# Latent queries projected in six blocks of 128 rows, the turned rows once, multiplied by cosine and sine as they leave PSUM

## The chip, the cores and the metric

The kernel runs on one core of one Trainium2 chip, alone. The metric is the device time of one execution in microseconds (us), the median of several runs. Three runs of the kernel before took 1103.07, 1103.22 and 1104.04 us, so the median is 1103.22.

Five engines work side by side, each through its own list of instructions in a fixed order: PE multiplies matrices (its weight loads are listed as PEld), DVE and ACT do work on whole tiles, POOL issues DMAs and a few small operations, SP issues DMAs. An instruction that needs a result of another engine waits on a semaphore, and everything behind it on its own engine waits too.

## What is computed

A trunk of two layers over 512 tokens of width 1024, in float32; each layer is a mixer followed by a gated FFN with a short convolution. The change touches the first layer's latent attention (MLA), which has 8 heads. Of each head's 96 query columns 64 are used as they are ("nope") and 32 are turned by the rotary embedding:

```python
def rope(x, pos):
    half = x.shape[-1] // 2
    ...
    x1, x2 = xf[..., :half], xf[..., half:]
    return jnp.concatenate([x1 * cos - x2 * sin, x2 * cos + x1 * sin], axis=-1)
...
q = heads_first(rms_norm(c_q, cq_g) @ w_uq, MLA_HEADS)
q_nope, q_rope = q[..., :MLA_NOPE], rope(q[..., MLA_NOPE:], pos)
kv = heads_first(rms_norm(c_kv, ckv_g) @ w_ukv, MLA_HEADS)
k_nope, v_mla = kv[..., :MLA_NOPE], kv[..., MLA_NOPE:]
o_mla = mla_attention(q_nope, q_rope, k_nope, rope(k_rope, pos), v_mla)
```

Scores are q_nope·k_nope + q_rope·k_rope, scaled by 96^-0.5, masked to the past, turned into shares by a softmax, and multiplied with the values. All heads share one turned key k_rope.

## The kernel before

Tokens are tiled in four blocks of 128 (`NT`), contraction dimensions in pieces of 128 (`P`). A product in float32 is made of three passes over split operands, high·high, high·low and low·high (`mm3`, lines 321 to 325): hence three rows, L323 to L325, for every product. Weights come in by DMA (`wraw`) and are split by ACT (`wh`, a cast, L84) and DVE (`wl`, a subtraction, L85); a split reuses the buffer of the weights split some steps earlier.

The first layer runs in stages. First the input projection makes, for each token, 256 latent query numbers, 128 latent key/value numbers and 32 key numbers to be turned (tile `ac`). A token-major tile `ctok` takes the normalised latents in its first three blocks of 128 columns; in the fourth it takes the turned key, four times over. PE transposes the four blocks into `tc`, and ACT and DVE split the first three into `cth` and `ctl` and put the turned key rows into `mk` (L1106 to L1109). Then the latent stage, the loop over `p2` (L1121 to L1142): in each of its four passes two heads' queries (`auq`), their keys (`auk`, 128 rows for two heads) and one token block of values (`auv`) are projected, each into a bank of PSUM under tag "a". Three banks have that tag, so a projection waits until an earlier one has been read out.

A head's query block before has 128 rows: 64 nope rows, the 32 rows to be turned, and the same 32 again with halves exchanged. DVE multiplies the whole block by a table `qtab` (one, cosine, sine, and the scale) as it leaves PSUM: one instruction for a head, L1128, eight in all, into `mq`. Score products run over 128 rows, and the key tile `mk` holds the turned key twice, so that cosine part and sine part add up in the product. In even heads the nope rows lie at 0 to 63, in odd heads at 64 to 127. ACT copies `auk` to `mk` (L1136, L1137, 64 rows each) and `auv` to `mv` (L1142).

The attention loop follows (L1226 to L1243): 16 units n, pair of heads p2 = n // 4, token block i = n % 4. For unit n PE makes two score tiles `sps` (L1151, the two banks of tag "s"); DVE adds the mask and takes the extreme (L1155); ACT takes exponentials (L1158); DVE takes reciprocals and scales (L1164, L1166); PE transposes the shares of unit n - 1 (`tpp`, L1178), DVE and ACT copy them out (L1189, L1187); after the last token block of a pair PE multiplies with the values (L1196). Between these, `plan` puts pieces of another projection, `av` for the differential attention (L1206, again tag "a"), on PE as a filler. In this loop the order on PE, DVE and ACT is as the code writes it; in the latent stage and ahead of it a scheduler sets the order of each engine when the kernel is built, and gives each projection one of the free banks.

Of the kernel before, what the change touches and what calls it, by code (L numbers as in the profile page):

```python
# [9 lines left out]
F32 = mybir.dt.float32  # L10
F32R = mybir.dt.float32r
BF16 = mybir.dt.bfloat16
AF = mybir.ActivationFunctionType
ALU = mybir.AluOpType
# [3 lines left out]
P = 128  # L18
S = 512
# [79 lines left out]
def trunk(tc, A, out):  # L99
# [3 lines left out]
    with ExitStack() as top:  # L103
# [103 lines left out]
        units += [(A["ev_w_uq"][u], 1024) for u in range(2)] + [(A["ev_w_ukv"], 1024)]  # L207
# [654 lines left out]
        def even():  # L862
            with ExitStack() as es:
# [43 lines left out]
                with ExitStack() as e1:  # L907
# [3 lines left out]
                    mv = mp.tile([P, NT, 512], F32, tag="mv", name="mv")  # L911
                    e2 = ExitStack()
# [152 lines left out]
                    with e2:  # L1065
                        qtab = cp.tile([P, 2, S], F32, tag="qtab", name="qtab")
# [11 lines left out]
                        for i in ORDER:  # L1078
# [4 lines left out]
                            for k in range(KD) if i < 2 else ():  # L1083
# [13 lines left out]
                            DVE.tensor_tensor(ctok[:, 3].rearrange("p (a b) -> p a b", a=4),  # L1097
                                              ra[:, 0:1].to_broadcast([P, 4, 32]),
                                              ra[:, 1:2].to_broadcast([P, 4, 32]), ALU.add)
# [9 lines left out]
                            ACT.copy(mk[1][0:64, t], tp[0:64, 3])  # L1109
# [10 lines left out]
                        kvh, kvl = W.next()  # L1120
                        for p2 in range(4):  # L1121
                            for z in range(2):
                                h = 2 * p2 + z
                                acc = bank("a", "auq")
                                for k in range(2):
                                    mm3(acc[:], uq[k][0][:, h * P:(h + 1) * P], uq[k][1][:, h * P:(h + 1) * P],
                                        ch[:, k], cl[:, k], k == 0, k == 1)
                                DVE.tensor_tensor(mq[h][:], acc[:], qtab[:, z], ALU.mult)  # L1128
                            he, ho = mk[2 * p2], mk[2 * p2 + 1]
                            if p2:  # L1130
                                DVE.tensor_copy(he[64:128, :], mk[0][64:128, :])
                                DVE.tensor_copy(ho[0:64, :], mk[1][0:64, :])
                            acc = bank("a", "auk")
                            mm3(acc[:], kvh[:, p2 * P:(p2 + 1) * P], kvl[:, p2 * P:(p2 + 1) * P],
                                ch[:, 2], cl[:, 2], True, True)
                            ACT.copy(he[0:64, :], acc[0:64, :])  # L1136
                            ACT.copy(ho[64:128, :], acc[64:128, :])  # L1137
                            i = p2
                            t = slice(i * P, (i + 1) * P)
                            acc = bank("a", "auv")  # L1140
                            mm3(acc[:], ch[:, 2, t], cl[:, 2, t], kvh[:, 512:], kvl[:, 512:], True, True)
                            ACT.copy(mv[:, i], acc[:])  # L1142
# [77 lines left out]
                    scored, left = {}, []  # L1220

# [4 lines left out]
                    with tc.manual_schedule(engines={PE.engine, DVE.engine, ACT.engine}):  # L1226
                        for n, (before, behind) in enumerate(plan):
# [9 lines left out]
                            if n < len(units):  # L1237
                                shares(scored[n])
                            fill(behind)
# [694 lines left out]
def layout(inputs):  # L1934
# [23 lines left out]
    nope, x1, x2 = uq[:, :, :64], uq[:, :, 64:80], uq[:, :, 80:]  # L1958
    even = np.concatenate([nope, x1, x2, x2, x1], 2)
    odd = np.concatenate([x1, x2, x2, x1, nope], 2)  # L1960
    uq = np.where((np.arange(8) % 2 == 0)[None, :, None], even, odd)
    r["ev_w_uq"] = uq.reshape(2, P, 1024)
# [36 lines left out]
    te = np.concatenate([one, c2.T, s2.T], 0) * sc  # L1999
    to = np.concatenate([c2.T, s2.T, one], 0) * sc  # L2000
    r["rope_q"] = np.stack([te, to], 1).astype(f)
# [32 lines left out]
```

## Time and profile before

| what | value |
|---|---|
| runs | 1103.07, 1103.22, 1104.04 us |
| profiled execution, first to last instruction (span) | 1101.2 us |
| median of the runs less that span | 2.0 us |
| PE: first query block of the latent stage starts | 42.65 us |
| PE: first filler product `av` starts | 59.64 us |
| PE: first score product of the next attention starts | 113.45 us |

The profile gives the profiled execution by its span alone; times in it are us from the start of the span. A timeline row reads: start, duration, engine, line, operation, out<-in, shape, count; in brackets the idle time of the engine in front of it and what ended that. A row with x2 or more merges instructions that follow each other.

### The profile page before, as it was taken

The numbers are of one execution on the slowest core, as the hardware profiler recorded it, in microseconds if no ns is written. First come the engines' busy times: TensorE is split into PE (matmuls) and PEld (weight loads), VectorE is DVE, ScalarE is ACT, GpSimd is POOL, SyncE is SP. The second block draws the span as 40 slices with busy tenths as digits, with TensorE's granted clock in tenths as the row PEclk, the third lists the DMA queues.
The fourth block names the chain that finished last, engine by engine and source line by source line (L and its number), as shares of the span: only waits on it lengthen the run. The fifth ranks groups of instructions, "written<-read, shape, count | busy, mean of one in ns | idle before, by whom it ended". The sixth has DMA issues, their size and how long they took to land.

```text
span 1101.2 us, 18064 instructions
## 1 busy us (share of the span) xinstructions
PE 1092.6 (99%) x6736; PEld 957.5 (87%) x6736; DVE 902.1 (82%) x1519; ACT 647.2 (59%) x1104; POOL 127.9 (12%) x246
## 2 busy tenths in 40 slices
PE   9999999999999999999999999999999999999997
PEld 8876788898999999888888877789999999988886
DVE  6766786498999999998974765468899999999896
ACT  6555676346666665556644654555566666656562
POOL 3211134220000000000032111114100000000002
PEclk9999999999999999999999999999999999999999
DMA  7897898467555555345618999867655555535462
GB/s 275 257 246 217 217 307 230 115 185 203 171 184 192 178 180 178 125 162 172 233 56 286 271 298 301 242 181 237 199 165 192 174 182 183 188 119 180 142 203 77
DMA packets 72601, 217.51 MB, mean 198 GB/s; under 512 B 10049, under 2 KB 11201, under 8 KB 64321
## 3 DMA queue, kind: packets, MB, share of 16 engines
q1 hardware_dynamic: 61872, 147.99, 40.2%
q0 software_dynamic: 9920, 67.12, 24.0%
q10 hardware_dynamic: 720, 1.25, 0.4%
q8 instruction: 53, 0.87, 0.3%
q14 instruction: 36, 0.29, 0.1%
HBM read 208.95 MB, written 73.43 MB: 256 GB/s over the span
## 4 chain that ended last, share of the span: by engine, by line
PE 96%; DVE 2%; ACT 1%; issue 0%; POOL 0%; POOLq 0%; DVEq 0%; ACTq 0%
PE u L325 12%; PE u L324 12%; PE u L323 12%; PE acc L324 6%; PE acc L323 6%; PE acc L325 6%; PE apt L323 3%; PE apt L324 3%; PE apt L325 3%; PE ao L323 2%; PE ao L325 2%; PE ao L324 2%; PE aqk L323 1%; PE p L325 1%; PE p L324 1%; PE p L323 1%
## 5 line engine op out<-in xcount | busy, mean ns | idle before, releaser
L85 DVE TENSOR_TENSOR wl<-wraw,wh 128x1024 fp32r<-128x1024 f32 x246 | 298.2, 1219 | 36.9 <-ACT wh L84 36.6
L84 ACT CAST wh<-wraw 128x1024 fp32r<-128x1024 f32 x246 | 254.3, 1046 | 100.1 <-PE u L324 22.1
L325 PE MATMUL u<-xh,wl 128*128 128x256 f32 (+1 forms) x640 | 194.9, 305 | 0.0
L324 PE MATMUL u<-xl,wh 128*128 128x256 f32 (+1 forms) x640 | 194.7, 304 | 0.0
L323 PE MATMUL u<-xh,wh 128*128 128x256 f32 (+1 forms) x640 | 194.5, 305 | 0.0
L325 PEld LDWEIGHTS u<-xh,wl 128*128 128x128 f32 x640 | 122.3, 191 | 5.5 <-DVE wl L85 0.7
L324 PEld LDWEIGHTS u<-xl,wh 128*128 128x128 f32 x640 | 122.3, 191 | 4.9
L323 PEld LDWEIGHTS u<-xh,wh 128*128 128x128 f32 x640 | 122.2, 191 | 5.0
L323 PE MATMUL u<-gh,wh 128*128 128x256 f32 x384 | 108.7, 283 | 0.0
L325 PE MATMUL u<-gh,wl 128*128 128x256 f32 x384 | 108.6, 283 | 0.0
L324 PE MATMUL u<-gl,wh 128*128 128x256 f32 x384 | 108.6, 283 | 0.0
L324 PE MATMUL acc<-wl,gh 128*128 128x512 f32 (+1 forms) x234 | 90.8, 388 | 0.0
L325 PE MATMUL acc<-wh,gl 128*128 128x512 f32 (+1 forms) x234 | 90.7, 387 | 0.0
L323 PE MATMUL acc<-wh,gh 128*128 128x512 f32 (+1 forms) x234 | 90.2, 388 | 0.0
L236 POOL TENSOR_TENSOR rv<-ms,epst 128x1 f32<-128x1 f32 x31 | 12.4, 399 | 615.6 <-ACT junk L290 285.0
L487 ACT ACTIVATE y<-u,cw 128x512 f32<-128x512 f32 x88 | 67.5, 776 | 27.2 <-PE u L325 27.2
L324 PEld LDWEIGHTS u<-gl,wh 128*128 128x128 f32 x384 | 73.7, 192 | 0.1
L323 PEld LDWEIGHTS u<-gh,wh 128*128 128x128 f32 x384 | 73.6, 192 | 0.1
L325 PEld LDWEIGHTS u<-gh,wl 128*128 128x128 f32 x384 | 73.7, 192 | 0.0
L164 POOL DMA_DIRECT2D ws<-in_ffn_up_q x72 | 51.5, 720 | 154.9 <-DMA ws<-ws 77.5
L493 DVE SCALAR_TENSOR_TENSOR y<-u,cw,y 128x510 f32<-128x510 f32 x88 | 65.6, 747 | 2.2
L491 DVE SCALAR_TENSOR_TENSOR y<-u,cw,y 128x511 f32<-128x511 f32 x88 | 65.1, 743 | 0.0
(391 smaller groups left out, 2475.6 us busy)
## 6 DMA issues: line engine op xcount, KB each, us to landing
ws<-in_ffn_up_q POOLq DMA_DIRECT2D x48, 768.0 KB, 12.9
wraw<-ws SPq DMA_DIRECT2D x128, 256.0 KB, 2.9
wraw<-in_ffn_up_q SPq DMA_DIRECT2D x96, 256.0 KB, 2.9
wraw<-in_ffn_w_down SPq DMA_DIRECT2D x44, 512.0 KB, 3.5
ws<-ws POOLq DMA_DIRECT2D x16, 768.0 KB, 13.3
ws<-in_ffn_up_q POOLq DMA_DIRECT2D x24, 512.0 KB, 6.3
wraw<-in_ffn_w_up SPq DMA_DIRECT2D x24, 512.0 KB, 4.4
wraw<-in_od_w_dqk SPq DMA_DIRECT2D x12, 512.0 KB, 9.6
```

The source lines that it names most:

```text
L84: self.nc.scalar.copy(h[:, :w], raw[:, :w])
L85: self.nc.vector.tensor_tensor(l[:, :w], raw[:, :w], h[:, :w].bitcast(F32), ALU.subtract)
L164: nc.gpsimd.dma_start(tiles[j][c][:].rearrange(wide, q=4), src.rearrange(wide, q=4), accum_op=op, max_dma_last_dim=8192)
L236: POOL.tensor_tensor(v[:, :n], ms, eps[:, :n], ALU.add)
L323: PE.matmul(o, lh, rh, start=first, stop=False, skip_group_check=more)
L324: PE.matmul(o, lh, rl, start=False, stop=False, skip_group_check=more)
L325: PE.matmul(o, ll, rh, start=False, stop=last, skip_group_check=more)
L487: ACT.activation(y[:, z], u[z], AF.Identity, bias=c[:, 3:4], scale=c[:, 2:3])
L491: DVE.scalar_tensor_tensor(y[:, z, 1:], u[z][:, :S - 1], c[:, 1:2], y[:, z, 1:], ALU.mult, ALU.add)
L493: DVE.scalar_tensor_tensor(y[:, z, 2:], u[z][:, :S - 2], c[:, 0:1], y[:, z, 2:], ALU.mult, ALU.add)
```

## The change

Query rows are laid out in six blocks of 128 in place of eight: for four heads together, two blocks that hold 64 nope rows, the 32 rows to be turned of that head and the 32 of a head two further on, and one block with the nope rows of two heads. The rows to be turned are projected once. DVE multiplies them twice, by the cosine into rows 64 to 95 of `mq` and by the sine into rows 96 to 127; the key tile has the turned key and, below it, the turned key with halves exchanged (one more small copy by ACT into `ctok` for each token block). All heads now have nope rows at 0 to 63. The nope block is taken out by ACT with the scale. For the second four heads ACT copies the two blocks to `q_late` in SBUF, and the eight DVE multiplications of these run inside the attention loop, one in each of units 0, 1, 2, 4, 5, 6, 8 and 9. `qtab` and `q_late` lie in buffers that the first layer's later attention uses afterwards.

```diff
@@ -204,7 +204,7 @@
         units = []
         units += [(A["ev_w_c"][u], 832) for u in range(4)]
         units += [(A["ev_w_dqk"][0, 0], 1024), (A["ev_w_dqk"][0, 1], 1024)]
-        units += [(A["ev_w_uq"][u], 1024) for u in range(2)] + [(A["ev_w_ukv"], 1024)]
+        units += [(A["ev_w_uq"][u], 768) for u in range(2)] + [(A["ev_w_ukv"], 1024)]
         units += [(A["ev_w_dv"][u], 1024) for u in range(4)]
         for h in range(1, 4):
             units += [(A["ev_w_dqk"][h, z], 1024) for z in range(2)]
@@ -909,6 +909,8 @@
                     mq = [mp.tile([P, S], F32, tag=f"mq{h}", name=f"mq{h}") for h in range(8)]
                     mk = [mp.tile([P, S], F32, tag=f"mk{h}", name=f"mk{h}") for h in range(8)]
                     mv = mp.tile([P, NT, 512], F32, tag="mv", name="mv")
+                    qtab, q_late = [ap.tile([P, 2, S], F32, tag=f"dqk{n}", name=name)
+                                    for n, name in ((2, "qtab"), (3, "q_late"))]
                     e2 = ExitStack()
                     cp = e2.enter_context(tc.tile_pool(name="ec", bufs=1, reuse_waits="tile"))
                     cgain = cp.tile([P, 384], F32, tag="cgain", name="cgain")
@@ -1063,7 +1065,6 @@
                         split_qk()
 
                     with e2:
-                        qtab = cp.tile([P, 2, S], F32, tag="qtab", name="qtab")
                         cT = (cp.tile([P, 3, S], F32R, tag="cth", name="cth"),
                               cp.tile([P, 3, S], F32R, tag="ctl", name="ctl"))
                         wc = [W.next() for _ in range(4)]
@@ -1094,9 +1095,10 @@
                                                      ALU.mult, ALU.mult)
                             DVE.scalar_tensor_tensor(ra[:, 1, 16:32], a[:, 384:400], ri, rtab[:, i, 1, 16:32],
                                                      ALU.mult, ALU.mult)
-                            DVE.tensor_tensor(ctok[:, 3].rearrange("p (a b) -> p a b", a=4),
-                                              ra[:, 0:1].to_broadcast([P, 4, 32]),
-                                              ra[:, 1:2].to_broadcast([P, 4, 32]), ALU.add)
+                            DVE.tensor_tensor(ctok[:, 3, 0:96].rearrange("p (a b) -> p a b", a=3),
+                                              ra[:, 0:1].to_broadcast([P, 3, 32]),
+                                              ra[:, 1:2].to_broadcast([P, 3, 32]), ALU.add)
+                            ACT.copy(ctok[:, 3, 96:128], ctok[:, 3, 16:48])
                             DVE.scalar_tensor_tensor(cf[:, 0:256], a[:, 0:256], rq[:, 0:1], cgain[:, 0:256],
                                                      ALU.mult, ALU.mult)
                             DVE.scalar_tensor_tensor(cf[:, 256:384], a[:, 256:384], rk[:, 0:1], cgain[:, 256:],
@@ -1106,7 +1108,6 @@
                                 PE.transpose(tp[:, k], ctok[:, k], ident[:])
                             split(cT[0][:, :, t], cT[1][:, :, t], tp[:, 0:3])
                             ACT.copy(mk[0][64:128, t], tp[64:128, 3])
-                            ACT.copy(mk[1][0:64, t], tp[0:64, 3])
                         row = bank("o", "row")
                         for i in range(NT):
                             PE.transpose(row[:, i * P:(i + 1) * P], r_tok[:, i:i + 1].to_broadcast([P, P]), ident[:])
@@ -1118,23 +1119,46 @@
                         ch, cl = cT
                         uq = [W.next() for _ in range(2)]
                         kvh, kvl = W.next()
+                        turned_q = []
+
+                        def q_block(g, b):
+
+                            acc = bank("a", "auq")
+                            c = slice((3 * g + b) * P, (3 * g + b + 1) * P)
+                            for k in range(2):
+                                mm3(acc[:], uq[k][0][:, c], uq[k][1][:, c], ch[:, k], cl[:, k], k == 0, k == 1)
+                            h = 4 * g + b
+                            if b == 2:
+                                for z in range(2):
+                                    ACT.activation(mq[h + z][0:64, :], acc[z * 64:(z + 1) * 64, :], AF.Copy,
+                                                   scale=-(96 ** -0.5))
+                                return
+                            src = acc
+                            if g:
+                                src = q_late[:, b]
+                                ACT.copy(src, acc)
+                            lo, hi = slice(64, 96), slice(96, 128)
+                            steps = [lambda o=o, r=r, n=n: DVE.tensor_tensor(o, src[r], qtab[r, n], ALU.mult)
+                                     for o, r, n in ((mq[h][0:96, :], slice(0, 96), 0), (mq[h][hi, :], lo, 1),
+                                                     (mq[h + 2][lo, :], hi, 0), (mq[h + 2][hi, :], hi, 1))]
+                            if g:
+                                turned_q.append(steps)
+                            else:
+                                for step in steps:
+                                    step()
+
                         for p2 in range(4):
-                            for z in range(2):
-                                h = 2 * p2 + z
-                                acc = bank("a", "auq")
-                                for k in range(2):
-                                    mm3(acc[:], uq[k][0][:, h * P:(h + 1) * P], uq[k][1][:, h * P:(h + 1) * P],
-                                        ch[:, k], cl[:, k], k == 0, k == 1)
-                                DVE.tensor_tensor(mq[h][:], acc[:], qtab[:, z], ALU.mult)
+                            for b in ((0, 1), (2, ))[p2 % 2]:
+                                q_block(p2 // 2, b)
                             he, ho = mk[2 * p2], mk[2 * p2 + 1]
-                            if p2:
-                                DVE.tensor_copy(he[64:128, :], mk[0][64:128, :])
-                                DVE.tensor_copy(ho[0:64, :], mk[1][0:64, :])
+                            for x in (he, ho):
+                                if x is not mk[0]:
+                                    DVE.tensor_copy(x[64:128, :], mk[0][64:128, :])
                             acc = bank("a", "auk")
                             mm3(acc[:], kvh[:, p2 * P:(p2 + 1) * P], kvl[:, p2 * P:(p2 + 1) * P],
                                 ch[:, 2], cl[:, 2], True, True)
                             ACT.copy(he[0:64, :], acc[0:64, :])
-                            ACT.copy(ho[64:128, :], acc[64:128, :])
+                            ACT.copy(ho[0:64, :], acc[64:128, :])
                             i = p2
                             t = slice(i * P, (i + 1) * P)
                             acc = bank("a", "auv")
@@ -1218,6 +1242,7 @@
                     units = [(p2, i) for p2 in range(4) for i in range(NT)]
                     plan = [(3, 0), (1, 0), (1, 0), (2, 0)] + [(3, 0), (0, 1), (1, 0), (2, 0)] * 3 + [(2, 2), (0, 0)]
                     scored, left = {}, []
+                    late_q = [turned_q[b][n] for n in range(4) for b in range(2)]
 
                     def fill(n):
                         for _ in range(n):
@@ -1236,6 +1261,8 @@
                                 turn(*units[n - 1], scored.pop(n - 1)[0])
                             if n < len(units):
                                 shares(scored[n])
+                            if n in (0, 1, 2, 4, 5, 6, 8, 9):
+                                late_q.pop(0)()
                             fill(behind)
                             if n == 8:
                                 W.ahead(W.pos + 1)
@@ -1955,11 +1982,10 @@
     r["ev_w_dqk"] = np.stack([cols(w[:, 416:928], P), cols(w[:, 928:1440], P)], 1)
     r["ev_w_dv"] = rows(w[:, 1440:], 2)
     uq = a["ev_w_uq"][0].reshape(256, 8, 96)
-    nope, x1, x2 = uq[:, :, :64], uq[:, :, 64:80], uq[:, :, 80:]
-    even = np.concatenate([nope, x1, x2, x2, x1], 2)
-    odd = np.concatenate([x1, x2, x2, x1, nope], 2)
-    uq = np.where((np.arange(8) % 2 == 0)[None, :, None], even, odd)
-    r["ev_w_uq"] = uq.reshape(2, P, 1024)
+    nope, turn = uq[:, :, :64], uq[:, :, 64:]
+    r["ev_w_uq"] = np.concatenate([part for h in (0, 4) for part in (
+        nope[:, h], turn[:, h], turn[:, h + 2], nope[:, h + 1], turn[:, h + 1], turn[:, h + 3],
+        nope[:, h + 2], nope[:, h + 3])], 1).reshape(2, P, 768)
     ukv = a["ev_w_ukv"][0].reshape(P, 8, 2, 64)
     r["ev_w_ukv"] = ukv.transpose(0, 2, 1, 3).reshape(P, 1024)
     r["ev_w_out"] = rows(a["ev_w_out"][0], 1)
@@ -1996,9 +2022,9 @@
     r["rope_tok"] = np.stack([c2, s2], 1).reshape(NT, P, 2, 32).transpose(1, 0, 2, 3).astype(f)
     sc = -(96 ** -0.5)
     one = np.ones((64, S))
-    te = np.concatenate([one, c2.T, s2.T], 0) * sc
-    to = np.concatenate([c2.T, s2.T, one], 0) * sc
-    r["rope_q"] = np.stack([te, to], 1).astype(f)
+    tc = np.concatenate([one, c2.T, c2.T], 0) * sc
+    ts = np.concatenate([one, -s2.T, -s2.T], 0) * sc
+    r["rope_q"] = np.stack([tc, ts], 1).astype(f)
     p = np.arange(P)[:, None]
     dist = p - (np.arange(S)[None, :] - 384)
     r["mla_mask"] = np.where(dist >= 0, 0.0, BIG).astype(f)
```

The order of instructions, at three places. A number behind a name tells buffers of one name apart; `mq0` to `mq7` are the heads' query tiles, `mk0` to `mk7` their key tiles.

PE, first pass of the latent stage, before: keys, values, then the next head's queries (`sps`, the score product, comes only after the whole stage).

```order
L323 MATMUL auk_696<-cth_353,wh_595 128x512
L324 MATMUL auk_696<-ctl_354,wh_595 128x512
L325 MATMUL auk_696<-cth_353,wl_596 128x512
L323 MATMUL auv_702<-wh_595,cth_353 128x512
L324 MATMUL auv_702<-wl_596,cth_353 128x512
L325 MATMUL auv_702<-wh_595,ctl_354 128x512
L323 MATMUL auq_707<-cth_353,wh_369 128x512
```

The same place in the change:

```order
L323 MATMUL auk_704<-cth_354,wh_596 128x512
L324 MATMUL auk_704<-ctl_355,wh_596 128x512
L325 MATMUL auk_704<-cth_354,wl_597 128x512
L1175 MATMUL sps_794<-mk0_125,mq0_117 128x128
L323 MATMUL auv_710<-wh_596,cth_354 128x512
L324 MATMUL auv_710<-wl_597,cth_354 128x512
L325 MATMUL auv_710<-wh_596,ctl_355 128x512
L323 MATMUL auq_715<-cth_354,wh_370 128x512
```

The first score product of head 0 has moved into the stage, between keys and values; that of head 1 stands at the same place of the second pass.

ACT, end of the latent stage and first exponential of the attention loop, before (`wh` are the last weights that `av` needs):

```order
L1142 COPY mv_133<-auv_760 128x512
L84 CAST wh_670<-wraw_668 128x1024
L84 CAST wh_676<-wraw_674 128x1024
L1136 COPY mk6_131<-auk_783 64x512
L1137 COPY mk7_132<-auk_783 64x512
L1142 COPY mv_133<-auv_789 128x512
L1158 ACTIVATE s_805,st_804<-s_805,st_804 128x128
```

The same place in the change:

```order
L1139 COPY q_late_135<-auq_737 128x512
L1139 COPY q_late_135<-auq_745 128x512
L1160 COPY mk4_129<-auk_755 64x512
L1161 COPY mk5_130<-auk_755 64x512
L1166 COPY mv_133<-auv_761 128x512
L84 CAST wh_671<-wraw_669 128x1024
L84 CAST wh_677<-wraw_675 128x1024
L1133 ACTIVATE mq6_123<-auq_766 64x512
L1133 ACTIVATE mq7_124<-auq_766 64x512
L1160 COPY mk6_131<-auk_777 64x512
L1161 COPY mk7_132<-auk_777 64x512
L1166 COPY mv_133<-auv_783 128x512
```

Two copies are new in front of the casts, and behind them two instructions that read the last query block, `auq_766`.

DVE, units 0 and 1 of the attention loop, in the change (before, the rows with `q_late` are not there, and the others stand in the same order; ISA rows are the masking step and its result):

```order
L1190 TENSOR_SCALAR s_799<-s_799,st_798 128x128
L1190 TENSOR_SCALAR s_800<-s_800,st_798 128x128
L1141 TENSOR_TENSOR mq4_121<-q_late_135,qtab_134 96x512
L1179 ISA s_824,st_823<-sps_819,mmask_381 128x256
L1179 ISA st_823 128x1
L1179 ISA s_825,st_823<-sps_820,mmask_381 128x256
L1179 ISA st_823 128x1
L1213 COPY pt_833<-tpp_834 128x128
L1188 RECIPROCAL st_823<-st_823 128x2
L1190 TENSOR_SCALAR s_824<-s_824,st_823 128x256
L1190 TENSOR_SCALAR s_825<-s_825,st_823 128x256
L1141 TENSOR_TENSOR mq5_122<-q_late_135,qtab_134 96x512
```

The late multiplication of unit n stands between the scaling of unit n's shares and the masking of unit n + 1.

## Prediction

> **What bounds the kernel now.** I read the page first: the engines' busy time and the chain of work that ended last, by engine.
>
> ```profile
> span 1101.2 us, 18064 instructions
> PE 1092.6 (99%) x6736; PEld 957.5 (87%) x6736; DVE 902.1 (82%) x1519; ACT 647.2 (59%) x1104; POOL 127.9 (12%) x246
> PE 96%; DVE 2%; ACT 1%; issue 0%; POOL 0%; POOLq 0%; DVEq 0%; ACTq 0%
> ```
>
> PE is busy throughout and carries the end. So a microsecond of PE work removed is a microsecond gained, and a microsecond in which PE stands waiting is one lost that nothing later gives back. Next I read the windows of the two stages that the change touches, the latent stage and the first part of the attention loop (columns: window, length, then busy us of PE, PEld, DVE, ACT, POOL, the granted clock, two columns on DMA).
>
> ```profile
> 42.40:59.30 16.90, 16.90 (x75) 13.64 (x74) 8.36 (x12) 8.91 (x14) 3.82 (x5) 1.00 1.03 283
> 59.30:80.00 20.70, 20.70 (x108) 15.17 (x107) 14.90 (x56) 11.22 (x38) 2.63 (x4) 1.00 0.97 256
> ```
>
> In the latent stage DVE and ACT are half idle. In the loop DVE has 14.90 of 20.70 us of work, in a fixed order between PE's waits: there a late instruction can hold PE. The clock is full in both, so durations can be carried over. All that follows is a replay of the two stages from the timeline's rows, with the changed order of each engine.
>
> **What is removed.** Before, eight query blocks are 48 passes; now six are 36.
>
> ```profile
> 42.65 0.39 PE L323 MATMUL auq<-cth,wh 128*128 128x512 f32 x1
> 45.37 0.39 PE L323 MATMUL auk<-cth,wh 128*128 128x512 f32 x1
> 45.46 1.28 DVE L1128 TENSOR_TENSOR mq<-auq,qtab 128x512 f32<-128x512 f32 x2
> 46.19 0.19 PEld L323 LDWEIGHTS auv<-wh,cth 128*128 128x128 f32 x1 [0.40 <-DVE mq L1128]
> 46.25 0.58 ACT L1136 COPY mk<-auk 64x512 f32<-64x512 f32 x1 [2.05 <-PE auk L325]
> 46.85 0.58 ACT L1137 COPY mk<-auk 64x512 f32<-64x512 f32 x1
> 47.00 0.39 PE L323 MATMUL auq<-cth,wh 128*128 128x512 f32 x1
> 48.59 0.69 DVE L1128 TENSOR_TENSOR mq<-auq,qtab 128x512 f32<-128x512 f32 x1 [1.85 <-PE auq L325]
> ```
>
> Twelve passes of two blocks take 45.37 - 42.65 = 2.72 us, 0.227 each; the twelve that go are worth -2.72 us if PE then never waits more than before. A block is 1.36, a projection of keys or values 0.68.
>
> **Latent stage, passes 0 and 1.** PE leaves the keys of pass 0 at 46.05 (45.37 + 0.68) in both kernels. Behind them now stands a score product of head 0, which needs the first copy to `mk` (ends 46.83) and DVE's second step on that head (two steps from 45.46, about 1.4 us: 46.85); so PE waits until 46.9, and the product takes about 0.18. The values need the bank of the keys, that is ACT's second copy, which ends at 47.43. They start at 47.48 and, with the restart that the wait of 0.40 shows above (46.20 to 47.00 for three passes), end at 48.28; before, PE was there at 47.00. Pass 1 has one query block (1.38 to 49.66), keys (0.68) and the score product of head 1: 50.52. The values then need the bank of the nope block, which ACT empties in two ACTIVATEs of 64x512. No such row exists before; the nearest are the 64x512 copy, 0.58 above, and an ACTIVATE of the same length on 128 rows:
>
> ```profile
> 86.96 0.67 ACT L1212 ACTIVATE dv<-av,lead 128x512 f32<-128x512 f32 x1
> ```
>
> 0.58 and 0.67 are the bounds; I take 0.67, since it is the same operation from PSUM. The block is ready at 49.87, two of them with gaps end at 51.23, the values run from 51.28 to 52.08 after a wait of 0.76. Passes 2 and 3 are 3 x 1.36 + 4 x 0.68 = 6.80 us without a wait on a bank: PE is through at 58.88.
>
> **The entry of the loop.** It is decided by ACT.
>
> ```profile
> 57.21 2.00 ACT L84 CAST wh<-wraw 128x1024 fp32r<-128x1024 f32 x2 [0.71 <-PE auq L324]
> 59.12 0.57 ACT L1136 COPY mk<-auk 64x512 f32<-64x512 f32 x1
> 59.28 0.60 PE L1151 MATMUL sps<-mk,mq 128*128 128x128 f32 x4
> 59.64 0.48 PE L323 MATMUL av<-wh,xh 128*128 128x512 f32 x1
> 60.31 0.59 ACT L1142 COPY mv<-auv 128x512 f32<-128x512 f32 x1
> 61.33 0.41 ACT L1158 ACTIVATE s<-s,st 128x128 f32<-128x128 f32 x1 [0.43 <-DVE st L1155]
> ```
>
> Now the keys of pass 2 are ready at 55.69 (52.08 + 2.72 + 0.68 + 0.2); ACT's copies to `mk4`, `mk5` and `mv` (0.58 + 0.58 + 0.59) end at 57.47. The two casts follow, 1.91 from start to next start (59.12 - 57.21): 59.38. Only then come the two ACTIVATEs on the last query block, 0.69 + 0.67: 60.74. The bank of that block is what the first `av` takes, so `av` starts at 60.79 against 59.64: **+1.15 us**, although PE was through at 58.88 and the score products at 59.28 have moved forward. The 2.72 us go into waits of 1.91 here, 0.76 in pass 1 and 1.28 in pass 0 (the moved product among them). With 0.58 an ACTIVATE, it is +0.8.
>
> ACT then still has the copies to `mk6`, `mk7` and `mv`; the first exponential comes at 62.54 against 61.33, 1.21 late, and DVE's first scaling with it.
>
> **The late multiplications.** Eight instructions enter DVE's list in the loop. Lengthwise they are 512, as L1128: fewer rows made ACT's copy no cheaper (0.58 on 64 rows, 0.59 on 128, above), so 0.69 each. What one costs behind another is less, for they overlap: two L1128 take 1.28, so the second adds 0.59 and I take 0.61 with its gap. That holds where both start at row 0, as in units 0 and 1 (96x512). The other six write 32 rows from row 64 or 96, amid instructions from row 0. Rows for that are DVE's copies of 64 rows, alternating between rows 64 to 127 (L1131) and 0 to 63 (L1132):
>
> ```profile
> 36.80 0.42 DVE L1131 COPY mk<-mk 64x512 f32<-64x512 f32 x1 [0.33 <-ACT mk L1108]
> 37.24 0.42 DVE L1132 COPY mk<-mk 64x512 f32<-64x512 f32 x1
> ```
>
> These start 0.44 apart and last 0.42: no overlap. So I take 0.77 for those six, 0.69 and the 0.08 of overlap lost in front; the bounds are 0.61 and 0.77. [...]
>
> What is behind a late step on DVE is the masking of the next unit (L1155), which frees the bank for PE's next score product; PE waits for that. Slack is where the product would have started anyway after the masking that it needs.
>
> ```profile
> 62.84 0.42 DVE L1155 CUSTOM_DVE_ANT_0 s<-sps,mmask 128x256 f32<-128x256 f32 x1
> 63.56 1.46 PE L1151 MATMUL sps<-mk,mq 128*128 128x384 f32 x4
> 65.16 0.55 DVE L1155 CUSTOM_DVE_ANT_0 s<-sps,mmask 128x384 f32<-128x384 f32 x1
> 65.97 1.88 PE L1151 MATMUL sps<-mk,mq 128*128 128x512 f32 x4
> 68.57 0.68 DVE L1155 CUSTOM_DVE_ANT_0 s<-sps,mmask 128x512 f32<-128x512 f32 x1
> 69.72 0.61 PE L1151 MATMUL sps<-mk,mq 128*128 128x128 f32 x4
> 72.87 0.76 DVE L1189 COPY pt<-tpp 128x256 f32<-128x256 f32 x2 [0.40 <-PE tpp L1178]
> 76.73 0.29 DVE L1189 COPY pt<-tpp 128x128 f32<-128x128 f32 x1 [1.83 <-PE tpp L1178]
> 78.19 0.56 DVE L1155 CUSTOM_DVE_ANT_0 s<-sps,mmask 128x384 f32<-128x384 f32 x1 [0.44 <-PE sps L1151]
> 83.06 0.68 DVE L1155 CUSTOM_DVE_ANT_0 s<-sps,mmask 128x512 f32<-128x512 f32 x1
> 83.53 0.77 PE L1151 MATMUL sps<-mk,mq 128*128 128x128 f32 x4
> 89.14 1.23 DVE L85 TENSOR_TENSOR wl<-wraw,wh 128x1024 fp32r<-128x1024 f32 x1 [0.94 <-ACT wh L84]
> 97.53 0.68 DVE L1155 CUSTOM_DVE_ANT_0 s<-sps,mmask 128x512 f32<-128x512 f32 x1
> 97.67 1.10 PE L1151 MATMUL sps<-mk,mq 128*128 128x128 f32 x4
> ```
>
> - n = 0: DVE is 1.21 + 0.61 = 1.82 late. The product at 63.56 could have gone at 63.31 (62.84 + 0.42 + 0.05), slack 0.25; PE, 1.15 late already, loses 1.82 - 0.25 - 1.15 = 0.42. PE late 1.57.
> - n = 1: DVE 2.43 late; slack 65.97 - 65.76 = 0.21; PE loses 0.65, late 2.22.
> - n = 2: DVE 3.20 late. The second product of the pair at 69.72 starts about 69.90, and the masking in front of it is over at 69.30: slack 0.60, PE loses 0.38, late 2.60.
> - n = 3 has no late step. At n = 4 DVE, 0.60 behind PE, gets 0.40 back by its idle time ahead of 72.87, and 1.83 ahead of 76.73 take the rest and the step: nothing.
> - n = 5: 0.77 less the idle 0.44 ahead of 78.19 leaves DVE 0.33 behind. n = 6: 1.10 behind, and the product at 83.53 has no slack (its second needs 83.06 + 0.68 + 0.05 = 83.79). PE loses 1.10, late 3.70.
> - n = 8: idle 0.94 ahead of 89.14 takes 0.77. n = 9: the masking at 97.53 ends after the next product's start at 97.67, so the step comes through whole: 0.77, late 4.47.
>
> The sum: -2.72 for the passes, +3.87 of waits up to the first `av` less what moved forward (1.15 net), +3.32 in the loop (0.42 + 0.65 + 0.38 + 1.10 + 0.77): **+4.5 us**. At 0.61 each, units 2, 6 and 9 lose 0.22, 0.78 and 0.61, and the sum is +3.8.
>
> **The rest.** Each token block gets a small ACT copy into `ctok` in place of one copy from `tc`, an exchange of like for like:
>
> ```profile
> 26.62 0.26 ACT L1108 COPY mk<-tc 64x128 f32<-64x128 f32 x1
> ```
>
> It now stands ahead of PE's last transpose of the block, and behind it queue ACT's splits. PE has filler products of another projection there, and ACT is idle about 40% of the span; I take 0, with bounds 0 and 4 x 0.26 = 1.0 us. Loads of the query weights shrink by a quarter; no wait for a load stands in the rows of this stage: 0.
>
> **The rivals.**
> 1. *The late steps are hidden* (0.12). DVE has 5.8 us free in the second window, and if the scaling's wait for ACT, not DVE's own length, sets each masking, the steps fall into idle time. Against it: the slacks above are 0.2 to 0.6 and idle time in front of the masks is small. Then only the entry remains: +1.15, 1104.4 us.
> 2. *Fewer rows cost less: no slower* (0.05). One price decides, that of an instruction on 64 or 32 rows. If it goes by rows, an ACTIVATE takes about 0.35, a late step 0.52 on 96 rows and 0.2 on 32. From 0.35 down the wait of pass 1 is gone (49.87 + 0.70 is when PE arrives), `av` starts at 59.4, 0.25 early, the first exponential 0.2 early; in the loop unit 1 loses 0.5 and units 6 and 9 lose 0.2 each: +0.9, 1104.1 us. Against it: 0.58 on 64 rows and 0.59 on 128.
> 3. *The token stage loses too* (0.06): PE has nothing else when a transpose waits for its `ctok` copy, 1.0 more: 1108.7 us.
> 4. *The saving is kept: faster* (0.08). If no new wait holds PE, neither `av` behind 58.88 nor a score product, -2.7 is left: 1100.5 us. For it speaks only that slacks of a few tenths decide units 0 to 2; against it ACT's list, on which casts of 1.9 us stand ahead of what `av` needs.
>
> **How the numbers follow.** The sum is made on the profiled execution, 1101.2 us; the median of the runs stands 2.0 above that span, and I carry this over: a span of 1105.7, a time of 1103.22 + 4.5 = 1107.7 us. Chance of the forecast 0.69. Its own range is 1106.3 to 1109.4: below, ACTIVATEs at 0.58 (-0.35) and all late steps at 0.61 (-0.7) and a little slack unseen; above, the 1.0 of the token stage and 0.7 for restarts after new waits. To take in rivals 1 to 3 the range runs from 1104.0 to 1109.4. What can be told from no change is 0.2%, 2.2 us. Rival 4 alone is faster: 0.08; rivals 1 and 2 lie within: 0.17; the forecast and rival 3 are slower: 0.75.
>
> **What will show it.** In the changed profile: the first `av` at about 60.8 with an idle time of about 1.9 in front of it, released by ACT's `mq`; the values of pass 1 held some 0.8 by the same; the first exponential at 62.5. PE late by 2.2 at unit 2's scores, by 3.7 in unit 8, and the next attention's first score product at about 118:
>
> ```profile
> 113.45 0.50 PE L1296 MATMUL sps<-dqk 64*128 64x512 f32 x2
> ```
>
> Late steps of 32x512 last 0.69. The forecast is wrong if `av` starts before 59.6, or if PE's lateness does not grow between 61 and 98 us.

## The result: slower by 0.47%

| | before | changed |
|---|---|---|
| median of five runs | 1103.58 us | 1108.41 us |
| lowest and highest | 1103.07, 1105.28 | 1107.97, 1110.41 |
| span of the profiled execution | 1101.2 us | 1106.6 us |

The ratio is 1.0047, its 95% interval 1.0036 to 1.0058. The predicted time was 1107.7 us, in a range from 1104.0 to 1109.4.

The page of the changed kernel (span, engines, chain of waits by engine) differs little from the one before. PE has 12 instructions fewer and is still busy for 99% of the span; a loss of 5 us does not show in shares.

```profile
span 1106.6 us, 18058 instructions
PE 1093.8 (99%) x6724; PEld 955.9 (86%) x6724; DVE 907.0 (82%) x1528; ACT 649.9 (59%) x1110; POOL 127.4 (12%) x246
PE 95%; DVE 2%; ACT 2%; issue 0%; POOL 0%; POOLq 0%; DVEq 0%; ACTq 0%
```

The window of the loop's first part tells more (same columns as in the prediction). PE works 18.63 of 20.70 us, where it had 20.70 before; DVE has 15.99 in place of 14.90.

```profile
59.30:80.00 20.70, 18.63 (x93) 12.91 (x92) 15.99 (x54) 11.84 (x37) 2.77 (x4) 1.00 0.98 259
```

The timeline of the changed kernel, at the places that the prediction named:

```profile
43.19 0.39 PE L323 MATMUL auq<-cth,wh 128*128 128x512 f32 x1
45.99 5.68 DVE L1141 TENSOR_TENSOR mq<-auq,qtab 96x512 f32<-96x512 f32 x8
47.52 0.46 PE L1175 MATMUL sps<-mk,mq 128*128 128x128 f32 x2 [0.77 <-DVE mq L1141]
50.55 1.20 ACT L1133 ACTIVATE mq<-auq 64x512 f32<-64x512 f32 x2 [0.94 <-PE auq L325]
51.80 0.50 PE L323 MATMUL auv<-wh,cth 128*128 128x512 f32 x1 [0.38 <-ACT mq L1133]
...
59.20 0.39 PE L325 MATMUL auv<-wh,ctl 128*128 128x512 f32 x1
61.05 0.50 PE L323 MATMUL av<-wh,xh 128*128 128x512 f32 x1 [1.46 <-ACT mq L1133]
...
118.34 0.50 PE L1323 MATMUL sps<-dqk 64*128 64x512 f32 x2
```

The waits stand where they were forecast: for DVE's second step in pass 0, for the nope block in pass 1, and 1.46 us in front of the first `av`. There PE has done its passes, twelve fewer than before, and waits for the last ACTIVATE. The chain of waits from the end of the stage (start, length, what) shows how the delay goes on:

```profile
58.96 0.71 ACT wh L84
59.81 0.59 ACT mq L1133
60.41 0.59 ACT mq L1133
61.03 0.58 ACT mk L1160
61.62 0.33 ACT mk L1161
61.95 0.28 issue
62.23 0.59 ACT mv L1166
62.81 0.78 ACT s L1182 x4
63.82 0.48 DVE s L1190 x2
64.30 0.60 DVE mq L1141
64.90 0.34 DVE s L1179
```

The path goes through ACT's casts, the ACTIVATEs, three copies and the first exponentials; then through DVE's scaling, and right behind it a late multiplication stands on it, ahead of the masking.

Three stretches divide the loss. The first product of the profiled execution started 0.29 later (7.13 us against 6.84), which the change does not touch; in the executions below this start lies anywhere between 6.70 and 7.21. The table leaves it out. All its numbers come from the timelines: start of the first transposes of `ctok`, of the first query pass, of the first `av`, and of the next attention's first score product.

| us | token stage | latent stage | attention loop | sum |
|---|---|---|---|---|
| before | 18.01 | 16.99 | 53.81 | 88.81 |
| changed | 18.28 | 17.86 | 57.29 | 93.43 |
| difference | +0.27 | +0.87 | +3.48 | +4.62 |

### The profile page after: what moved, and what is told of

Read it like the earlier page. It is cut to its first block, busy times and chain, and to the rows that moved or that the text cites. A ratio compares the mean times of both kernels' runs of the same rounds, so it can differ in the third digit from the quotient of the medians.

```text
span 1106.6 us, 18058 instructions
## 1 busy us (share of the span) xinstructions
PE 1093.8 (99%) x6724; PEld 955.9 (86%) x6724; DVE 907.0 (82%) x1528; ACT 649.9 (59%) x1110; POOL 127.4 (12%) x246
## 4 chain that ended last, share of the span: by engine, by line
PE 95%; DVE 2%; ACT 2%; issue 0%; POOL 0%; POOLq 0%; DVEq 0%; ACTq 0%
PE u L325 12%; PE u L324 12%; PE u L323 12%; PE acc L323 6%; PE acc L324 6%; PE acc L325 6%; PE apt L323 3%; PE apt L324 3%; PE apt L325 3%; PE ao L323 2%; PE ao L325 2%; PE ao L324 2%; PE aqk L323 1%; PE p L325 1%; PE p L324 1%; PE p L323 1%
```

## The experiments

All start from the changed kernel. Ratios are to the kernel before, timed in the same round, each with its 95% interval. Times also move by one to two us with what happens behind these stretches (last section), so the three stretches are read beside them. In diffs and listings, `...` stands for lines left out.

**Six passes put back.** If ACT holds the entry, PE has room there.

```diff
                             acc = bank("a", "auv")
+                            if p2 == 3:
+                                for _ in range(2):
+                                    mm3(acc[:], ch[:, 2, t], cl[:, 2, t], kvh[:, 512:], kvl[:, 512:], True, True)
                             mm3(acc[:], ch[:, 2, t], cl[:, 2, t], kvh[:, 512:], kvl[:, 512:], True, True)
```

> Six passes of 128x512 that change no result are put into PE's list ahead of the last value projection of the latent stage, behind the last query block: 6 x 0.227 = 1.36 us of PE work, half of what the change removed. Theory (the entry of the loop is decided by ACT; PE stands 1.46 us in front of the first av): they fill the wait. av stays at 61.05 us within 0.2, the next attention's first score product at 118.3, the time at 1108.4. Rival (PE's length decides): av comes 1.36 later and so does the end, 1109.8.

Measured: 1108.32 us, ratio 1.0042 (1.0027 to 1.0057). The last value pass and the first `av`, in its timeline:

```profile
60.64 0.39 PE L325 MATMUL auv<-wh,ctl 128*128 128x512 f32 x1
61.14 0.50 PE L323 MATMUL av<-wh,xh 128*128 128x512 f32 x1
```

The wait is filled with work, and `av` comes 17.88 us after the first query pass, as without it (17.86). Half of what the change took off PE can be put back at no cost. The rival is out.

**No late multiplications.** Those of heads 4 to 7 are left out; POOL fills their rows with zeros early.

```diff
+                        for m in mq[4:]:
+                            POOL.memset(m[:], 0.0)
...
-                            if n in (0, 1, 2, 4, 5, 6, 8, 9):
-                                late_q.pop(0)()
```

> The eight late multiplications are left out (their rows of the query tiles are filled with zeros by POOL ahead of the stage, so heads 4 to 7 have wrong scores). Theory (they delay the masking, which frees the bank for PE): what PE loses between the entry of the loop and the next attention, 4.89 - 1.45 = 3.4 us, vanishes; PE is some 1.4 us later than before at all score products, the next attention's first one at 114.9, the time about 1105.0. Rival (the loop loses by ACT's late exponentials and the banks, not by DVE's list): no more than 1 us of it goes, 1107.5 or above.

Measured: 1105.79 us, ratio 1.0018 (1.0009 to 1.0027). The timeline, with DVE in unit 2:

```profile
60.65 0.50 PE L323 MATMUL av<-wh,xh 128*128 128x512 f32 x1 [1.46 <-ACT mq L1135]
68.27 0.75 DVE L1192 TENSOR_SCALAR s<-s,st 128x384 f32<-128x384 f32 x2
68.94 0.68 DVE L1181 CUSTOM_DVE_ANT_0 s<-sps,mmask 128x512 f32<-128x512 f32 x1
114.54 0.49 PE L1323 MATMUL sps<-dqk 64*128 64x512 f32 x2
```

The wait in front of `av` is the same 1.46, and the loop takes 53.89 us (114.54 - 60.65) in place of 57.29, as before the change within 0.1. The eight steps cost 3.40 us, and the loop gives nothing of the late entry back. The time is 0.8 above the expected 1105.0; in the profiled execution the stretch behind the loop took 0.7 us longer than in the change, and no run shows why.

**Late multiplications from row 0.** Same lengths, but the six on 32 rows read and write rows 0 to 31.

```diff
+                        for m in mq[4:]:
+                            POOL.memset(m[64:128, :], 0.0)
...
+                            if g:
+                                r0 = slice(0, 32)
+                                steps[1:] = [lambda n=n: DVE.tensor_tensor(src[r0], src[r0], qtab[r0, n], ALU.mult)
+                                             for n in (1, 0, 1)]
```

> The six late multiplications on 32 rows keep their length but read and write rows 0 to 31 (in place in q_late; the rows of the query tiles that they no longer write are zero, so heads 4 to 7 have wrong scores). Theory (an instruction that starts in another group of 32 rows than its neighbour does not overlap with it): each costs DVE 0.60 in place of 0.82, and the next attention's first score product comes 0.5 to 0.8 us earlier, at 117.5 to 117.8. Rival (the start row changes nothing, 0.7 to 0.8 is the price of the instruction): 118.3 as in the change.

Measured: 1108.46 us, ratio 1.0038 (1.0024 to 1.0052); the loop 56.27 us, 1.02 less than in the change and more than the 0.5 to 0.8 that was expected. DVE in unit 2, scaling, step, masking; first in this kernel, then in the change:

```profile
69.57 0.75 DVE L1196 TENSOR_SCALAR s<-s,st 128x384 f32<-128x384 f32 x2
70.23 0.67 DVE L1148 TENSOR_TENSOR q_late<-q_late,qtab 32x512 f32<-32x512 f32 x1
70.83 0.67 DVE L1185 CUSTOM_DVE_ANT_0 s<-sps,mmask 128x512 f32<-128x512 f32 x1
117.02 0.49 PE L1329 MATMUL sps<-dqk 64*128 64x512 f32 x2
```

```profile
69.87 0.75 DVE L1190 TENSOR_SCALAR s<-s,st 128x384 f32<-128x384 f32 x2
70.65 0.68 DVE L1141 TENSOR_TENSOR mq<-q_late,qtab 32x512 f32<-32x512 f32 x1
71.36 0.69 DVE L1179 CUSTOM_DVE_ANT_0 s<-sps,mmask 128x512 f32<-128x512 f32 x1
```

From scaling to masking it is 1.26 us here, 1.49 in the change, and 0.67 without a step. A step that starts at its neighbours' row costs 0.59, one that does not 0.82. Here the step starts 0.66 after the start of the two scalings, which last 0.75, and the masking 0.60 after the start of the step, which lasts 0.67. In the change it is 0.78 after 0.75 and 0.71 after 0.68: no overlap in front of the step, and none behind it. The runs have starts at rows 0, 64 and 96 only; how far apart two starts must lie, the 32 rows of the theory included, they do not show. The medians do not show the gain of 1.02 (1108.46 against 1108.41): runs of one kernel scatter by more than a microsecond (1107.97 to 1110.41 in the change). The verdict on the start row rests on the loop.

**Copies of the first four heads' blocks too.** ACT takes them out of PSUM in one instruction each.

```diff
-                            src = acc
-                            if g:
-                                src = q_late[:, b]
-                                ACT.copy(src, acc)
+                            src = q_late[:, b]
+                            ACT.copy(src, acc)
```

> The first four heads' two blocks are copied to SBUF by ACT as well, in one instruction of 0.59 each, before DVE multiplies them; the banks come free 2 to 5 us sooner, and the two first score products stand behind the stage again. Theory (PE's waits of passes 0 and 1 are waits for banks and for DVE's steps): these waits, 1.28 and 0.76 in the prediction, are gone, PE is through the stage at 57.0 to 57.4 and the first av starts at 58.7 (61.05 in the change), the first exponential at 60.4; the time falls by about 2.3 us to 1106.1. Rival (ACT's list is full, two more copies of 0.59 come on top): av no earlier than 60.8, the time 1108.4 to 1109.6.

Measured: 1106.17 us, ratio 1.0019 (1.0009 to 1.0030).

```profile
57.11 0.60 PE L1174 MATMUL sps<-mk,mq 128*128 128x128 f32 x4
58.73 0.50 PE L323 MATMUL av<-wh,xh 128*128 128x512 f32 x1 [1.02 <-ACT mq L1133]
60.39 0.41 ACT L1181 ACTIVATE s<-s,st 128x128 f32<-128x128 f32 x1
116.02 0.49 PE L1322 MATMUL sps<-dqk 64*128 64x512 f32 x2
```

PE reaches the score products, now behind the stage, at 57.11; the first `av` comes 15.47 us after the first query pass (17.86 in the change). So 2.4 us of the lost gain lay in waits for banks and for DVE's first steps; the edit takes away both, and the two early score products with them, and does not tell them apart. The loop is untouched, 57.29. ACT still makes PE wait 1.02.

**Part of ACT's list given to DVE.** The copies to `mk4` and `mk5`, and the first half of the last nope block.

```diff
+                                    if g and z == 0:
+                                        DVE.tensor_scalar(o, a, -(96 ** -0.5), None, ALU.mult)
...
-                            ACT.copy(he[0:64, :], acc[0:64, :])
-                            ACT.copy(ho[0:64, :], acc[64:128, :])
+                            copy = DVE.tensor_copy if p2 == 2 else ACT.copy
+                            copy(he[0:64, :], acc[0:64, :])
+                            copy(ho[0:64, :], acc[64:128, :])
```

> Three ACT instructions at the end of the latent stage go to DVE, which is idle there: the copies to mk4 and mk5 and the first half of the last nope block. Theory (ACT's list decides the entry: casts of 2.0 us stand ahead of the two ACTIVATEs that av waits for): all that follows on ACT comes 1.1 to 1.2 us sooner; the first av starts 16.7 us after the first query pass (17.86 in the change, 16.99 before), the first exponential 18.4 after it (19.52 in the change), and this stays to the end: the time about 1107.2. Rival (PE itself or DVE's weight splits hold av): av moves by less than 0.3 and the time stays at 1108.4.

Measured: 1107.23 us, ratio 1.0033 (1.0021 to 1.0045).

```profile
59.42 0.59 ACT L1137 ACTIVATE mq<-auq 64x512 f32<-64x512 f32 x1
60.07 0.50 PE L323 MATMUL av<-wh,xh 128*128 128x512 f32 x1 [0.47 <-ACT mq L1137]
61.72 0.40 ACT L1186 ACTIVATE s<-s,st 128x128 f32<-128x128 f32 x1
117.32 0.50 PE L1327 MATMUL sps<-dqk 64*128 64x512 f32 x2
```

The first `av` stands 16.86 us after the first query pass, the first exponential 18.51; both are 1.0 less than in the change, and the loop keeps its 57.25. ACT's list does decide the entry, and what is gained there stays.

**Late multiplications in the stage.** Five run in the latent stage, two in unit 4, one in unit 8.

```diff
-                            if g:
-                                turned_q.append(steps)
+                            if g and b:
+                                steps.pop(0)()
+                                turned_q.extend(steps)
...
-                    late_q = [turned_q[b][n] for n in range(4) for b in range(2)]
+                    late_q = turned_q
...
-                            if n in (0, 1, 2, 4, 5, 6, 8, 9):
+                            for _ in range({4: 2, 8: 1}.get(n, 0)):
                                 late_q.pop(0)()
```

> The eight late multiplications stay in, but five of them run in the latent stage, where DVE is idle from 51.7 to 59.0 us, straight behind ACT's copies, two in unit 4 and one in unit 8, where the change showed idle time of DVE. Theory (their place costs 3.4 us, not their work): from the first av to the next attention's first score product 53.8 to 54.3 us (57.29 in the change, 53.81 before), the time 1105.0 to 1105.8, as with the multiplications left out. Rival (the work costs wherever it stands, as DVE's weight splits and the masking of unit 0 come later): no more than half of it goes, 1106.7 or above.

Measured: 1105.20 us, ratio 1.0013 (1.0004 to 1.0023).

```profile
54.81 3.51 DVE L1141 TENSOR_TENSOR mq<-q_late,qtab 96x512 f32<-96x512 f32 x5 [3.13 <-ACT q_late L1139]
59.00 2.36 DVE L85 TENSOR_TENSOR wl<-wraw,wh 128x1024 fp32r<-128x1024 f32 x2 [0.68 <-ACT wh L84]
114.96 0.50 PE L1324 MATMUL sps<-dqk 64*128 64x512 f32 x2
```

DVE does the five in 3.51 us and is idle for 0.68 before the splits, which start at 59.00 as in the change. The loop takes 53.91, as if there were no late steps. All the work is done; its place in the change cost 3.4 us.

**Copies and place together.**

> Both edits together: all four turned blocks copied to SBUF by ACT, and the late multiplications in the stage but for three. Theory (waits for banks in the stage, -2.3, and DVE's list in the loop, -3.4, add up): first av 15.5 us after the first query pass as with the copies alone, 53.8 to 54.3 from there to the next attention, the time about 1102.7, 1 us under the kernel before. Rival (the gains overlap: with PE earlier, ACT's exponentials hold the loop): 1104 to 1105.

Measured: 1102.61 us, ratio 0.9991 (0.9982 to 1.0000). First `av` and next attention:

```profile
58.60 0.51 PE L323 MATMUL av<-wh,xh 128*128 128x512 f32 x1 [1.02 <-ACT mq L1133]
112.50 0.50 PE L1323 MATMUL sps<-dqk 64*128 64x512 f32 x2
```

The latent stage takes 15.44 us and the loop 53.90: the two gains add up. From the transposes of `ctok` to the next attention it is 87.59 us, 1.22 less than before the change. By the medians of its round this version is 0.95 us ahead of the kernel before (1103.56), but the interval reaches to 1.0000: that it is faster is not shown beyond doubt.

**With the nope block shared as well.**

> As with copies and stage together, and the first half of the last nope block goes to DVE, which was idle for 0.63 us there. ACT had no gap from 53.8 us to the first exponential, so theory (ACT's list still decides the entry): first av and first exponential 0.6 us sooner, 14.8 and 16.5 after the first query pass (15.44 and 17.10 without), 53.9 from there to the next attention, the time 0.6 lower, about 1102.0, or 0.15% under the kernel before. Rival (PE is through the stage by then, or DVE's weight splits come late and hold the masking): less than 0.2 of it.

Measured: 1103.52 us, ratio 0.9996 (0.9987 to 1.0005). First `av` and next attention:

```profile
58.12 0.50 PE L323 MATMUL av<-wh,xh 128*128 128x512 f32 x1 [0.54 <-ACT mq L1137]
112.06 0.50 PE L1326 MATMUL sps<-dqk 64*128 64x512 f32 x2
```

The first `av` comes 14.98 us after the first query pass and the first exponential 16.63, 0.46 and 0.47 sooner; the loop takes 53.94. That lies between the two expectations, nearer to the first. The time did not follow: 1102.0 was expected, and the interval overlaps that of the version without this edit, so the two times can't be told apart. The stretch behind the loop was longer in the profiled execution; the last section has what is known of it.

**The exchanged key halves by DVE.**

```diff
-                            ACT.copy(ctok[:, 3, 96:128], ctok[:, 3, 16:48])
+                            for c, d in ((96, 16), (112, 0)):
+                                DVE.tensor_tensor(ctok[:, 3, c:c + 16], ra[:, 0, d:d + 16], ra[:, 1, d:d + 16],
+                                                  ALU.add)
```

> The small copy by ACT into ctok is replaced by two additions of 128x16 on DVE, which make the exchanged halves directly. Theory (PE's last transpose of a token block waits for that copy): the stretch from the first transposes of ctok to the first query pass takes 18.0 us as before in place of 18.28, 0.27 less at the end. Rival (something else in the token stage, or DVE's two more instructions cost as much): 18.28 or more.

Measured: 1110.15 us, ratio 1.0055 (1.0041 to 1.0069). The edit regroups the transposes, so the stretch is read from PE's product ahead of them to the first query pass: the rows of before, of the change, and two of this kernel.

```profile
20.55 0.46 PE L325 MATMUL ac<-wh,xl 128*128 128x416 f32 x1 [0.20 <-DVE xl L949]
```

```profile
20.83 0.46 PE L325 MATMUL ac<-wh,xl 128*128 128x416 f32 x1 [0.19 <-DVE xl L951]
```

```profile
20.56 0.46 PE L325 MATMUL ac<-wh,xl 128*128 128x416 f32 x1 [0.19 <-DVE xl L951]
42.60 0.39 PE L323 MATMUL auq<-cth,wh 128*128 128x512 f32 x1
```

To the first query pass (42.65, 43.19, 42.60) it takes 22.10, 22.36 and 22.04 us. Without ACT's copy the token stage is back at its length, as expected. Yet the kernel came out slower than the change, which no theory expected. Its latent stage (17.86) and its loop (57.31) are as in the change; the loss comes later. In the profiled execution, the slowest of the four, the stretch behind the loop took 991.8 us against 988.3 in the change. One wait of PE in it, at the place that the last section describes, is this; the rest of the cause was not settled.

```profile
763.25 1.23 PE L271 MATMUL tp<-ident,t 128*128 128x128 f32 x8 [1.38 <-DVE t L1916]
```

## Why the prediction was right, step by step

- *Pass 0.* Right. With the stage's later start (43.19 against 42.65, 0.54), the moved product was forecast at 47.44 and the values at 48.02; they came at 47.52 and 48.02.
- *Pass 1.* The place was right, the wait 0.38 in place of 0.76: PE's second moved product started 0.16 later than forecast and took 0.38, not 0.18. The values began at 51.80, where 51.82 was forecast, because two errors cancel: ACT began the ACTIVATEs 0.14 later (50.55 against 49.87 + 0.54 = 50.41), and the two took 1.20 in place of 1.36.
- *Entry.* Right in its cause, shown by the passes put back and by giving part of ACT's list to DVE; too large in size. An ACTIVATE of 64x512 takes 0.59, near the lower bound, not 0.67; the row from which 0.67 came reads a second operand, `lead`, which these do not, but no run separates what that costs. Two ACTIVATEs make 0.17 of the 0.28 between +1.15 and +0.87; the other 0.11 is that the last copy and the casts overlap (57.43 + 0.59 against 57.91). The wait shrank further, to 1.46 from 1.91, because PE was through the stage 0.17 later than forecast (16.40 after its first query pass, not 16.23). The first exponential came 0.84 late in place of 1.21.
- *The loop.* +3.48 against a forecast of +3.32, and 3.40 of it goes with the steps. The size of a step on 32 rows was slightly low: 0.82, not 0.77. The forecast has no overlap on either side of the step, but puts the starts right at the ends; the rows show some 0.03 between end and start on each side (69.87 + 0.75 to 70.65, 70.65 + 0.68 to 71.36). By the timelines PE's score products grow later by 0.29, 0.64, 0.10, 0.41, 0, 0, 0.81, 0.33, 0, 0.37 and 0.46 us from unit 2 to unit 12. The forecast had 0.42 for the step of unit 0, 0.65 for unit 1, 0.38 for unit 2, 1.10 for unit 6 and 0.77 for unit 9: the later three came in two parts each, over two products (0.51, 1.14, 0.83). Units 4 and 8 cost nothing, as forecast.
- *The token stage.* Taken at 0 with a bound of 1.0; it costs 0.27, and taking ACT's copy away returns it. Rival 3 was right in kind, at a quarter of its size.
- *The rivals.* The late steps are not hidden (rival 1). Fewer rows do not cost less (rival 2): a late multiplication by DVE took 0.68 us on 32 and on 96 rows, and the multiplication before the change 0.69 on 128. As its terms stand, rival 2 comes to +0.65 (-0.25 + 0.5 + 0.2 + 0.2), not +0.9, unless unit 0 uses up the early start, which it does not say; either is far from what was measured. The saving is not kept (rival 4), but it is real: with the waits and the place mended, 1.2 us of it is there in the three stretches.

Against the predicted +4.5 us, +4.83 was measured between the medians (1108.41 - 1103.58), and +4.62 in the three stretches. That the sum comes so near is in part luck: its errors are -0.28 in the latent stage, +0.16 in the loop and +0.27 in the token stage. The mechanism does not rest on it; the experiments show it part by part.

## What to carry to other kernels

A saving on the engine that sets the end is worth nothing while another engine's list ends last at the next hand-over: write out that list up to the point where the bank comes free. Here the twelve passes saved went into waits, at the entry of the loop for two ACTIVATEs behind two casts, and in the first two passes of the stage for banks and for DVE's steps. Work that is put into a tightly woven loop costs where it stands straight ahead of what the critical engine waits for: eight steps of 0.68 us, spread over units of the loop, cost 3.40 us, though DVE was busy for only 15.99 of 20.70 us there. The same eight steps cost nothing with five of them in the idle stretch of the stage and three where DVE waited in the loop: it took 53.91 us, and 53.89 without any. Fewer rows saved nothing in DVE's multiplications (0.68 us on 32 and on 96 rows, 0.69 on 128) or ACT's copies (0.58 on 64, 0.59 on 128), and a step that starts at row 64 or 96, between neighbours at row 0, cost 0.82 in place of 0.59.

## What the runs showed that was not expected

The part of the kernel behind the loop has the same instructions in every version, and yet its length differs. From the next attention to the last instruction it is 987.8 us before, 988.3 in the change, 989.9 with the passes put back and 990.6 with the nope block shared. These are single executions, and the last two were slow ones among their own kernel's (1110.1, the slowest of four, and 1104.46 against a median of 1103.52). When the loop ends does not decide it alone: in the change and with the passes put back it ends within 0.1 us (118.34 and 118.43), and the rest differs by 1.6. Part of the difference is one place in the second layer, some 640 us behind the change. POOL's rows there, before and with the nope block shared, and PE's row of the latter:

```profile
752.72 0.60 POOL L164 DMA_DIRECT2D ws<-ws  x1 [3.16 <-DMA ws<-in_ffn_up_q]
753.34 0.21 POOL L236 TENSOR_TENSOR rv<-ms,epst 128x1 f32<-128x1 f32 x1
```

```profile
754.66 0.60 POOL L164 DMA_DIRECT2D ws<-ws  x1 [4.14 <-DMA ws<-in_ffn_up_q]
757.05 1.23 PE L271 MATMUL tp<-ident,t 128*128 128x128 f32 x8 [0.75 <-DVE t L1917]
```

POOL issues a DMA that waits for another one, and the small operations of a normalisation stand behind it in POOL's list. With the nope block shared the DMA went out 1.9 us later than before (754.66 against 752.72), although the loop had ended 1.4 earlier; the normalisation went with it, and PE waited 0.75 for its product. Of the eleven profiled executions, five have such a wait at this place, of 0.72 to 1.53 us, and their rest takes 989.5 to 991.8 us; the six without it, the kernel before and the change among them, take 987.8 to 989.0. So the wait goes with the longer rest, but it does not cover all of the difference. What makes the DMA late in one execution and not in another was not tested; that the earlier stage's timing shifts it is an inference.

A copy of 64x512 out of PSUM took 0.68 us on DVE (in the run that gave it part of ACT's list) and 0.58 on ACT, so work moved from ACT to DVE grew by a sixth.
